# A hybrid decoder layer on one core: side work placed by estimated engine clocks, and gate2 and x1 applied once at the end of the down projection

## The chip, the core and the metric

The kernel runs on one core of one Trainium2 chip. The metric is device time in microseconds (us). Engines are named as in the profile: PE is TensorE, whose weight loads are listed apart as PEld, DVE is VectorE, ACT is ScalarE, POOL is GpSimd, SP is SyncE, which issues most of the DMAs. The kernel before takes 3123.56 us (median of 3 runs, 3122.35 to 3125.27).

## The reference

One inference step of one layer, in float32, for a prompt of 2048 tokens and for 8 sample rows of one token each that share every weight:

```python
h = rmsnorm(x, norm1_g) * (1 + scale1) + shift1          # shift, scale, gate from silu(c) @ w_ada
z = h @ w_in                                             # D = 1024 to 2568 columns
y_a = chunk gating of gelu(z[..., :512]);  y_b = conformer conv of z[..., 512:1024]
y_c = forgetting attention of q, k, v = z[..., 1024:2560], 8 heads of 64
y = concat(rms(y_a), rms(y_b), rms(y_c)) * mix_g
x = x + gate1 * (y @ w_out)
h = rmsnorm(x, norm2_g) * (1 + scale2) + shift2
up = causal depthwise conv3(h @ w_up)                    # 1024 to 2 x 2816
x = x + gate2 * ((silu(up[..., :2816]) * up[..., 2816:]) @ w_down)
return rmsnorm(x, final_g), ...                          # and the new K, V, log-forget and conv rows
```

A sample row attends to 4096 past positions that lie in 32 pages of 128 positions; a page table says where.

## The kernel before

Every large product is made of three float32r matmuls: each operand is split in a high and a low part, and `mm3` (lines 80 to 86) adds high x high, high x low and low x high in PSUM. PSUM is handed out in three tiles `acc` of 128 x 1024 and two tiles `misc` of 128 x 512. The prompt goes in 4 chunks of 512 tokens.

Phase 1 runs, for each chunk, ten groups of columns of `w_in`. Weights come over SP's queue (`raw`), ACT makes the high part `wh`, POOL the low part `wl`. Beside the groups run small tasks, which are Python generators: `norm1` of the next chunk (16 transposes into four `acc` tiles, and for each of eight k a scaling `hmod` and a cast `hh` on ACT and a difference `hl` on DVE), the rest of the adaLN product (`ada_rest`, its weights `wada` issued from ACT's queue), layer norms, gating, row outputs. A task gives up with `yield`, and is taken up again at fixed points: `advance` calls each task once per group, and a number given with `yield` makes it miss so many turns.

Phase 2 is the prompt's attention. In its last quarter `norm_c` normalises the attention's output: squares, four matmuls against ones (128x1), a reciprocal root, four scalings of the identity, one matmul (128x512).

Phase 3 does w_out, norm2, up, down and the final norm, chunk by chunk. A chunk's up projection has 22 tiles of two pieces of weights (48 matmuls each), its down projection has four parts, of 6, 6, 4 and 6 of these tiles. A part is two halves of 512 columns, each with two `acc` tiles. `up` ends a tile with the conv's taps on DVE (four `uy<-ub`, one `uy<-uy`) and the split into `ah` (ACT) and `al` (DVE), which `down` uses as its stationary side. After each half `down` multiplies the sum by gate2 and adds it to `xa`, which holds x1 from the start.

Between them the sample rows' attention goes on. A page step of `logits` (lines 1163 to 1169) takes two pages of K from a ring of four `pg` buffers that SP's queue fills: a product with the query (DVE, `pg<-pg,qb`), a sum by heads (DVE, `red<-pg`), and an addition into the logits `S`. There are 16 steps for each of 8 rows. `values` then takes the maximum, the exponential and the sum (matmuls against `mx`, `dg`, `lsum`) and multiplies 16 x 2 pages of V (tiles `yv` and `pg`) with 32 columns each. How many steps go where is set by numbers: `bg(2)` gives two units of credit, each step costs what its `yield` says, and values of row s-1 and logits of row s take turns.

In a row, L1164 and the like name the line in the listing.

## Time and profile before

| what | value |
|---|---|
| median of 3 runs | 3123.56 us |
| the profiled execution | 3115.85 us, of which 3113.7 us are the span from first to last instruction |
| mean granted PE clock | 0.975 |
| busy share of the span | PE 95%, PEld 69%, DVE 67%, POOL 43%, ACT 39% |
| DMA | 523.90 MB, mean 168 GB/s |

All rows below come from the profiled execution. Busy shares are means over the span: phase 1 ends near 610 us, phase 2 near 1181 us, and the sample rows' page steps stand between 1249 and 2373 us. A wait is idle time of an engine just before an instruction, with what ended it. The granted clock of PE has two levels, 2.4 GHz (1.00) and 1.2 GHz (0.50).

### The profile page before, as it was taken

What the parts mean: (1) busy time and instruction counts of PE and PEld (TensorE: products, weight loads), DVE (VectorE), ACT (ScalarE), POOL (GpSimd) and SP (SyncE); (2) the same over time, 40 slices, a digit from 0 to 9 for tenths busy, and PEclk for the clock granted to TensorE, in tenths of its full rate; (3) what the DMA queues carried; (4) which work ended last, traced back from release to release, by engine and by line L of the source; (5) the groups of instructions that cost most, each with busy time, mean ns of one, the idle gap of its engine ahead of it and who ended that gap; (6) DMA issues with size and microseconds to landing.
All of it is one profiled execution on the core that took longest, in us unless ns stands there. A gap on an engine that the chain in (4) does not pass through costs nothing. (4 is left out here: it accounts for less than half of the span.)

```text
span 3113.7 us, 41614 instructions
## 1 busy us (share of the span) xinstructions
PE 2951.6 (95%) x14352; PEld 2151.2 (69%) x14352; DVE 2087.9 (67%) x2767; ACT 1228.0 (39%) x1717; POOL 1338.4 (43%) x884
## 2 busy tenths in 40 slices
PE   7998989899999989989999999999999999999998
PEld 4776768765555547767776767777767776777775
DVE  4838384858777763986887968785958554645454
ACT  4453535233333343434335433443433433534333
POOL 3544354423333444544444444454444454344443
PEclk9999999999999979999999999999999999999999
DMA  8355756563412327766677787678866627322222
GB/s 260 108 181 171 238 174 205 150 176 80 95 44 63 99 81 281 226 209 200 200 220 236 220 246 212 206 220 284 261 185 191 177 79 235 111 82 82 82 82 78
DMA packets 443589, 523.90 MB, mean 168 GB/s; under 512 B 35111, under 2 KB 281173, under 8 KB 443362
## 3 DMA queue, kind: packets, MB, share of 16 engines
q1 hardware_dynamic: 414418, 478.25, 51.3%
q10 hardware_dynamic: 28672, 41.95, 4.0%
q8 instruction: 113, 1.85, 0.2%
q0 software_dynamic: 288, 1.05, 0.1%
q14 instruction: 98, 0.80, 0.1%
HBM read 453.08 MB, written 68.38 MB: 167 GB/s over the span
## 5 line engine op out<-in xcount | busy, mean ns | idle before, releaser
L1525 POOL TENSOR_TENSOR wl<-raw,wh 128x1024 fp32r<-128x1024 f32 x296 | 769.3, 2609 | 874.9 <-ACT wh L1524 841.9
L84 PE MATMUL acc<-hh,wh 128*128 128x512 f32 x1792 | 721.0, 403 | 3.1 <-ACT hh L451 2.1
L85 PE MATMUL acc<-hl,wh 128*128 128x512 f32 x1792 | 709.4, 396 | 1.8 <-DVE hl L452 1.3
L86 PE MATMUL acc<-hh,wl 128*128 128x512 f32 x1792 | 709.1, 396 | 0.1
L1524 ACT CAST wh<-raw 128x1024 fp32r<-128x1024 f32 x296 | 308.8, 1047 | 552.9 <-PE acc L86 163.7
L1692 DVE SCALAR_TENSOR_TENSOR uy<-ub,fw,uy 128x512 f32<-128x512 f32 x352 | 282.8, 851 | 234.0 <-ACT uy L1689 232.6
L84 PEld LDWEIGHTS acc<-hh,wh 128*128 128x128 f32 x1792 | 338.2, 189 | 127.7 <-issue 22.0
L86 PEld LDWEIGHTS acc<-hh,wl 128*128 128x128 f32 x1792 | 338.4, 189 | 81.5 <-POOL wl L1525 1.0
L85 PEld LDWEIGHTS acc<-hl,wh 128*128 128x128 f32 x1792 | 338.6, 189 | 79.4 <-DVE hl L452 2.1
L496 POOL TENSOR_TENSOR wl<-raw,wh 128x512 fp32r<-128x512 f32 (+1 forms) x160 | 240.1, 1520 | 205.8 <-ACT wh L495 168.7
L84 PE MATMUL acc<-wh,ah 128*128 128x512 f32 x752 | 310.6, 413 | 16.0 <-ACT ah L1698 11.1
L86 PE MATMUL acc<-wh,al 128*128 128x512 f32 x752 | 303.6, 404 | 1.6 <-DVE al L1699 1.6
L85 PE MATMUL acc<-wl,ah 128*128 128x512 f32 x752 | 303.1, 403 | 1.0 <-POOL wl L1525 1.0
L963 POOL TENSOR_TENSOR lsum<-lsum,pt 128x512 f32<-128x512 f32 x96 | 141.0, 1469 | 203.8 <-PE misc L965 102.5
L676 DVE SCALAR_TENSOR_TENSOR cv<-glu,convw,cv 128x512 f32<-128x512 f32 x240 | 226.0, 1004 | 0.0
L1164 DVE TENSOR_TENSOR pg<-pg,qb 128x1024 f32<-128x1024 f32 x128 | 198.4, 1552 | 36.0 <-DMA pg<-in_cache_k 32.7
L995 ACT ACTIVATE pt<-acc 128x1024 f32<-128x1024 f32 (+2 forms) x144 | 126.9, 883 | 240.0 <-PE acc L993 182.5
L84 PEld LDWEIGHTS acc<-wh,ah 128*128 128x128 f32 x752 | 145.7, 194 | 77.1 <-issue 23.9
L84 PE MATMUL acc<-wh,hh 128*128 128x256 f32 (+2 forms) x552 | 163.4, 296 | 9.2 <-DVE nm L871 7.2
L86 PEld LDWEIGHTS acc<-wh,al 128*128 128x128 f32 x752 | 145.3, 193 | 37.9 <-DVE al L1699 3.9
L869 DVE TENSOR_REDUCE nm<-acc 128x1 f32<-128x1024 f32 (+1 forms) x128 | 121.5, 950 | 71.8 <-PE acc L864 71.1
L85 PEld LDWEIGHTS acc<-wl,ah 128*128 128x128 f32 x752 | 145.8, 194 | 32.8 <-POOL wl L1525 1.4
(382 smaller groups left out, 4836.9 us busy)
## 6 DMA issues: line engine op xcount, KB each, us to landing
raw<-in_w_up SPq DMA_DIRECT2D x176, 512.0 KB
pg<-in_cache_k SPq DMA_DIRECT2D x256, 256.0 KB
raw<-in_w_down SPq DMA_DIRECT2D x88, 512.0 KB
yv<-in_cache_v SPq DMA_DIRECT2D x138, 256.0 KB
raw<-in_w_in SPq DMA_DIRECT2D x132, 256.0 KB
pg<-in_cache_v SPq DMA_DIRECT2D x118, 256.0 KB
wada<-in_w_ada ACTq DMA_DIRECT2D x64, 256.0 KB
raw<-in_w_out SPq DMA_DIRECT2D x32, 512.0 KB
```

The source lines that it names most:

```text
L84: nc.tensor.matmul(out, lhsT=lh, rhs=rh, start=start, stop=False)
L85: nc.tensor.matmul(out, lhsT=lh, rhs=rl, start=False, stop=False)
L86: nc.tensor.matmul(out, lhsT=ll, rhs=rh, start=False, stop=stop)
L496: nc.gpsimd.tensor_tensor(out=wl[:, :, 0:n], in0=raw[:, :, 0:n], in1=f(wh[:, :, 0:n]), op=ALU.subtract)
L676: nc.vector.scalar_tensor_tensor(out=y[:, m, :], in0=glu[:, m, j:j + T], scalar=self.convw[:, m, j:j + 1], in1=y[:, m, :], op0=ALU.mult, o ...
L869: nc.vector.tensor_reduce(out=m1, in_=flat[:, 0:full], axis=AX.X, op=ALU.max, negate=True)
L963: e.tensor_tensor(out=lsum[:, i, off:], in0=lsum[:, i, off:], in1=pt[:, i, 0:T - off], op=ALU.add)
L995: nc.scalar.activation(out=pt[:, :, 0:w], in_=ps[:, :, 0:w], func=AF.Exp)
L1164: nc.vector.tensor_tensor(out=t, in0=t, in1=qs[s].unsqueeze(1).broadcast_to([P, 2, 512]), op=ALU.mult)
L1524: nc.scalar.copy(out=wh, in_=raw)
L1525: nc.gpsimd.tensor_tensor(out=wl, in0=raw, in1=f(wh), op=ALU.subtract)
L1692: nc.vector.scalar_tensor_tensor(out=y[:, i, :], in0=ub[:, i, s:s + T], scalar=self.fw[:, s, n:n + 1], in1=y[:, i, :], op0=ALU.mult, op1=A ...
```

## The change

Every engine is wrapped. After each instruction `Estimate.note` adds its estimated cost to a clock of its engine, starting no earlier than the estimated end of what it reads or overwrites; DMAs go to one clock at 280 GB/s. A task now yields a list of what it needs, and is taken up again when the estimate says that this is ready by PE's (or another engine's) clock. Page steps of K run ahead of the values by themselves; they are emitted as long as DVE's clock is less than `lag` behind PE's, 12 us mostly and 3 us in the last two tiles before a down part. `norm1` starts at n == 2 of each chunk as such a task, and what is left of it at the chunk's last group is run off there. The `wada` loads go over SP's queue. V pages use the `yy` ring while it is lent, and `pg` only when no K pages are left. The weights of the next pieces are split before a tile's taps. In the down projection part 0 copies the sum to `xa` (ACT), parts 1 to 3 add to it, and part 3 then multiplies by gate2 and adds x1, which is loaded again as `x1r`. The conformer's layer norm reads a copy in SBUF instead of PSUM.

```diff
+    def cost(self, e, op, outs, ins):
+        n = max(free(x) for x in outs + ins[:1])
+        if e == "tensor":
+            if op == "transpose":
+                return 0.11
+            n = free(ins[1])
+            if "float32r" in str(ins[1].dtype):
+                return max(0.107, 0.0045 + 0.000445 * n)
+            return 4 * max(0.045, 0.00042 * n) * min(1.0, outs[0].shape[0] / 128)
+        if e == "vector":
+            if op == "reciprocal":
+                return 0.1 + 0.0066 * n
+            sb = [x for x in ins if "PSUM" not in str(x.space) and free(x) > 1]
+            return (0.14 + 0.00105 * n) * (1.1 if len(sb) > 1 else 1.0)
+        if e == "scalar":
+            return 0.19 + 0.00083 * n
+        return (1.0 if n < 64 else 0.15) + 0.0023 * n
...
+    def ok(self, need, e="tensor"):
+
+        return not isinstance(need, list) or self.nc.ready(need) <= max(self.nc.t["tensor"], self.nc.t[e]) + 0.1
...
+    def tick(self, n=1):
+
+        for _ in range(n):
+            if self.ok(self.need):
+                self.need = next(self.side, None)
...
-            adas = c in (1, 2) and (c, n) >= (1, 2)
-            if adas:
-                next(ada, None)
+            if (c, n) == (1, 1):
+                self.later(ada)
...
-            if n >= 2:
-                next(nxt, None)
-            if adas:
-                next(ada, None)
+            if n == 2:
+                self.later(nxt)
...
-                self.nc.scalar.dma_start(out=w, in_=self.I["w_ada"][k * P:(k + 1) * P, c0:c0 + 512])
+                self.nc.sync.dma_start(out=w, in_=self.I["w_ada"][k * P:(k + 1) * P, c0:c0 + 512])
...
+    def more(self):
+
+        for _ in range(2):
+            if self.ok(self.wait, "vector"):
+                self.wait = next(self.sample_units, None)
...
             for g in range(NP // 2):
-                t = page()
+                more_k()
+                yield [kt[0], qs[s]]
+                t = kt.pop(0)
...
-            yield 2
+            yield [dg]
...
+        while kn or vs:
+            went = False
+            if vs and self.ok(vn):
+                went = True
+                try:
+                    vn = next(vs)
+                except StopIteration:
+                    vs = None
+            if kn and self.ok(kn, "vector") and (self.force or self.nc.t["vector"] < self.nc.t["tensor"] + self.lag):
+                went = True
+                kn = next(ks, None)
...
-        for _ in range(waits[1]):
-            yield
+        yield [sq, self.acc_free]
...
-                next(self.side, None)
-                if i == 0 and (j != tiles[-1] or len(out) != len(tiles) - 1):
-                    self.bg(2 if c or j > 2 else 0)
+                self.tick()
+                self.lag = 3 if j in tiles[-2:] and tiles[-1] in part else 12
+                if i == 0:
+                    self.more()
...
             for b2 in range(2):
-                t = p3.tile([P, 2, 512], F32, name="t", bufs=2)
-                nc.vector.tensor_tensor(out=t, in0=ps[b2], in1=self.gate[:, 1:2, ns].broadcast_to([P, 2, 512]), op=ALU.mult)
                 xa = self.xa[:, 2 * b2:2 * b2 + 2, ns]
-                nc.vector.tensor_tensor(out=xa, in0=xa, in1=t, op=ALU.add)
+                if n == 0:
+                    nc.scalar.copy(out=xa, in_=ps[b2])
+                else:
+                    nc.vector.tensor_tensor(out=xa, in0=ps[b2], in1=xa, op=ALU.add)
+                if last:
+                    nc.vector.tensor_tensor(out=xa, in0=xa, in1=self.gate[:, 1:2, ns].broadcast_to([P, 2, 512]), op=ALU.mult)
+                    nc.vector.tensor_tensor(out=xa, in0=xa, in1=x1[b2], op=ALU.add)
```

The order of instructions changes on every engine. Every instruction of the kernel after has line L100, that of the wrapper. Three places follow.

The first is ACT's order around norm1 of chunk 1, in phase 1. Before, `hmod` and `hh` of one transposed tile stand among the casts `wh` and outputs of the groups, one tile per group:

```order
L569 COPY sig<-acc 128x1024
L558 ACTIVATE sp_h<-acc 128x1024
L515 COPY zs<-misc 8x256
L561 DMA kh_d<-sp_h 128x2x512
L450 ACTIVATE hmod<-acc,modT,s_226 128x512 x2
L451 CAST hh<-hmod 128x512 x2
L506 COPY part<-misc 128x256
L495 CAST wh<-raw 128x2x256 x4
L558 ACTIVATE sp_h<-acc 128x1024
```

The same in the kernel after, from the output of the chunk's last group (`sp_h`, `qh_d`) on:

```order
L100 ACTIVATE sp_h<-acc 128x1024
L100 ACTIVATE hmod<-acc,modT,s_226 128x512
L100 DMA qh_d<-sp_h 128x2x512
L100 CAST hh<-hmod 128x512
L100 ACTIVATE hmod<-acc,modT,s_226 128x512
L100 CAST wh<-raw 128x2x256
L100 CAST hh<-hmod 128x512
L100 ACTIVATE hmod<-acc,modT,s_226 128x512
L100 COPY part<-misc 128x256
L100 CAST hh<-hmod 128x512
L100 ACTIVATE hmod<-acc,modT,s_226 128x512
L100 COPY zs<-misc 8x256
```

Three of the four tiles' `hmod` and `hh` now stand behind the last group's output, one after the other, where chunk 1's first group needs them.

The second is PE's order where phase 2 ends. Before, the last norm_c stands inside the last attention block, with scores (`acc<-q,k`) between its two steps:

```order
L965 MATMUL misc<-pt,v 64x512 x6
L1487 MATMUL acc<-ones,wk 128x1 x4
L992 MATMUL acc<-q_6414,k_6412 128x512
L993 MATMUL acc<-q_6415,k_6413 128x512
L992 MATMUL acc<-q_6414,k_6412 128x512
L993 MATMUL acc<-q_6415,k_6413 128x512
L1495 MATMUL acc<-wk,ones 128x512
```

After, it stands behind the last block, in front of w_out's first product (`acc<-wh,yy`):

```order
L100 MATMUL misc<-pt,v 64x128 x2
L100 MATMUL acc<-lsum,ones 64x512 x2
L100 MATMUL acc<-ones,wk 128x1 x4
L100 MATMUL acc<-wk,ones 128x512
L100 MATMUL acc<-wh,yy 128x512
L100 MATMUL acc<-wl,yy 128x512
```

Its two steps follow each other directly.

The third is DVE's order in part 2 of chunk 0's down projection, between the second sum of the first half and the first sum of the second. Before, the sums are `t<-acc,gate` and `xa<-xa,t`, and two page steps stand about them:

```order
L1760 TENSOR_TENSOR t<-acc,gate 128x1024
L1168 SCALAR_TENSOR_TENSOR S<-red,S 128x16
L1164 TENSOR_TENSOR pg<-pg,qb 128x1024
L1762 TENSOR_TENSOR xa<-xa,t 128x2x512
L1166 TENSOR_REDUCE red<-pg 128x16
L1168 SCALAR_TENSOR_TENSOR S<-red,S 128x16
L1164 TENSOR_TENSOR pg<-pg,qb 128x1024
L1166 TENSOR_REDUCE red<-pg 128x16
L1760 TENSOR_TENSOR t<-acc,gate 128x1024
```

After, 17 instructions of page steps stand between the two sums `xa<-acc,xa`, the last of them here:

```order
L100 TENSOR_TENSOR pg<-pg,qb 128x1024
L100 TENSOR_REDUCE red<-pg 128x16
L100 SCALAR_TENSOR_TENSOR S<-red,S 128x16
L100 TENSOR_TENSOR pg<-pg,qb 128x1024
L100 TENSOR_REDUCE red<-pg 128x16
L100 SCALAR_TENSOR_TENSOR S<-red,S 128x16
L100 TENSOR_TENSOR xa<-acc,xa 128x2x512
L100 TENSOR_TENSOR pg<-pg,qb 128x1024
L100 TENSOR_REDUCE red<-pg 128x16
L100 TENSOR_TENSOR xa<-acc,xa 128x2x512
```

Counted over DVE's order from the sixth to the 34th `al` (chunk 0's sixth up tile to chunk 1's twelfth), 62 page steps stand there before and 108 after. All 128 stand ahead of the 34th `al` after; before, the last stands behind the 54th.

## Rows read from the trace of the kernel before

**Rows 1.** The page's first part: engine, busy us, share, instructions.
```profile
PE 2951.6 (95%) x14352; PEld 2151.2 (69%) x14352; DVE 2087.9 (67%) x2767; ACT 1228.0 (39%) x1717; POOL 1338.4 (43%) x884
```
**Rows 2.** PE's waits, 60 to 620 us: us in total, times, longest.
```profile
PE misc L255 <- DMA wada<-in_w_ada: 17.2, 5, 7.0
...
PE acc L432 <- ACT vt L590: 5.8, 2, 4.2
PE misc L503 <- ACT part L506: 5.2, 1, 5.2
```
**Rows 3.** Four stretches at the low clock, their sum: length, busy us by engine.
```profile
sum 23.80, PE 14.33 PEld 4.66 DVE 5.19 ACT 20.94 POOL 15.05; mean PE 3.58 PEld 1.17 DVE 1.30 ACT 5.23 POOL 3.76
```
**Rows 4.** ACT's groups, 30 to 620 us: count, busy us, mean ns, idle before.
```profile
L451 ACT CAST hh<-hmod 128x512 fp32r<-128x512 f32 x32 | 19.2, 615 | 1.0 <-DVE hmod L448 0.6
L450 ACT ACTIVATE hmod<-acc,modT,s 128x512 f32<-128x512 f32 x24 | 18.3, 772 | 1.7 <-PE acc L432 1.4 <-ACT zs L515 0.3
```
**Rows 5.** PE's waits over the whole run, norm_c's first step.
```profile
PE acc L1487 <- DVE wk L1481: 7.7, 3, 3.0
```
**Rows 6.** Two stretches at the low clock, 1119.5 to 1140 and 1157 to 1170.7, their sum.
```profile
sum 34.20, PE 29.56 PEld 15.94 DVE 17.36 ACT 9.34 POOL 8.36; mean PE 14.78 PEld 7.97 DVE 8.68 ACT 4.67 POOL 4.18
```
**Rows 7.** PE in order of time, 1157 to 1162 us: start, length, instruction, idle before.
```profile
1157.40 1.84 PE L1487 MATMUL acc<-ones,wk 128*128 128x1 f32 x8 [2.98 <-DVE wk L1481]
...
1161.59 1.19 PE L1495 MATMUL acc<-wk,ones 128*128 128x512 f32 x1 [0.44 <-DVE wk L1491]
```
**Rows 8.** PE's waits, 1181 to 1373 us.
```profile
PE acc L84 <- ACT ah L1698: 7.2, 1, 7.2
```
**Rows 9.** One stretch: busy us (instructions) by engine, granted clock, DMA share, GB/s.
```profile
1365.20:1378.90 13.70, 7.13 (x16) 5.17 (x17) 9.35 (x10) 3.03 (x4) 5.18 (x3) 0.50 1.06 348
```
**Rows 10.** Five stretches between the 6th and the 34th `al`, 1372.9 to 1922.2 us, their sum.
```profile
sum 549.30, PE 532.66 PEld 396.59 DVE 435.83 ACT 220.41 POOL 246.52; mean PE 106.53 PEld 79.32 DVE 87.17 ACT 44.08 POOL 49.30
```
**Rows 11.** DVE's groups, 1372.9 to 1922.2 us.
```profile
L1164 DVE TENSOR_TENSOR pg<-pg,qb 128x1024 f32<-128x1024 f32 x62 | 96.3, 1556 | 27.7 <-DMA pg<-in_cache_k 24.4 <-DMA yv<-in_cache_v 3.3
L1166 DVE TENSOR_REDUCE red<-pg 128x16 f32<-128x1024 f32 x62 | 74.7, 1211 | 0.7
L1168 DVE SCALAR_TENSOR_TENSOR S<-red,S 128x16 f32<-128x16 f32 x61 | 43.6, 719 | 0.7
L1762 DVE TENSOR_TENSOR xa<-xa,t 128x1024 f32<-128x1024 f32 x20 | 32.4, 1619 | 0.2
...
L1760 DVE TENSOR_TENSOR t<-acc,gate 128x1024 f32<-128x1024 f32 x20 | 24.4, 1218 | 16.8 <-PE acc L86 16.8
```
**Rows 12.** A page step's three lines on DVE: ns min/median/max, first and last start.
```profile
L1164 DVE TENSOR_TENSOR pg<-pg,qb x128: 1204/1216/3432, 1249.3 to 2372.9; 128x1024 f32<-128x1024 f32 x128
...
L1166 DVE TENSOR_REDUCE red<-pg x128: 1196/1208/1222, 1258.0 to 2374.2; 128x16 f32<-128x1024 f32 x128
...
L1168 DVE SCALAR_TENSOR_TENSOR S<-red,S x128: 153/168/2416, 1260.3 to 2375.4; 128x16 f32<-128x16 f32 x128
```
**Rows 13.** PE's groups, 1330 to 2540 us: the products with V pages.
```profile
L1205 PE MATMUL misc<-yv,S 128*32 128x512 f32 x276 | 48.1, 598 | 0.1
L1205 PE MATMUL misc<-pg,S 128*32 128x512 f32 x236 | 45.9, 601 | 0.0
```
**Rows 14.** The page's groups: POOL's split of the weights in phase 3.
```profile
L1525 POOL TENSOR_TENSOR wl<-raw,wh 128x1024 fp32r<-128x1024 f32 x296 | 769.3, 2609 | 874.9 <-ACT wh L1524 841.9
```
**Rows 15.** PE's waits, 1922.2 to 3095 us.
```profile
PE misc L1184 <- DVE dg L1181: 7.3, 3, 3.9
...
PE misc L1191 <- DVE lsum L1188: 4.9, 1, 4.9
PE misc L1320 <- DVE ys L1314: 4.2, 1, 4.2
```
**Rows 16.** Four stretches at the low clock between 2273 and 2646 us, their sum.
```profile
sum 20.40, PE 17.11 PEld 14.01 DVE 11.76 ACT 6.75 POOL 10.29; mean PE 4.28 PEld 3.50 DVE 2.94 ACT 1.69 POOL 2.57
```

More of the change, by code (lines that the diff above doesn't have):

```diff
@@ L39, in f, with is_ap, free, __init__ @@
     return ap.bitcast(F32)
+def is_ap(x):
+    return type(x).__name__ == "AP"
+def free(ap):
+    n = 1
+    for _, m in list(ap.ap)[1:]:
+        n *= m
+    return n
+class State:
+    def __init__(self, since):
+        self.since, self.w, self.r, self.last = since, [], [], since
+    def span(self, ap):
+        step = ap.ap[0][0] or 1
+        lo = ap.offset % step if step > 1 else ap.offset
+        return lo, lo + sum((m - 1) * abs(q) for q, m in list(ap.ap)[1:]) + 1
+    @staticmethod
+    def after(items, lo, hi, e="none"):
+        return max((t for a, b, t, by in items if a < hi and lo < b and by != e), default=0.0)
+    def put(self, items, lo, hi, t, e):
+        items[:] = [x for x in items if x[3] != e or not (lo <= x[0] and x[1] <= hi)][-24:] + [(lo, hi, t, e)]
+        self.last = max(self.last, t)
@@ new lines, with __init__, tile, free_at @@
+class Ring:
+    def __init__(self, pool, est, bufs):
+        self.pool, self.est, self.bufs, self.made = pool, est, bufs, {}
+    def tile(self, shape, dtype, **kw):
+        t = self.pool.tile(shape, dtype, **kw)
+        made = self.made.setdefault(kw.get("tag") or kw["name"], [])
+        n = kw.get("bufs") or self.bufs
+        made.append(State(made[-n].last if len(made) >= n else 0.0))
+        self.est.tiles[t.tensor.name] = made[-1]
+        return t
+    def free_at(self, tag, n):
+        made = self.made.get(tag, [])
+        return made[-n].last if len(made) >= n else 0.0
@@ L318, in phase1 @@
                 if c == NCH - 1:
+                    for _ in ada:
+                        pass
+                    self.tasks = [t for t in self.tasks if t[0] is not ada]
                     for name in ("hta", "pa", "px"):
@@ L358, in fill @@
         next(self.filler, None)
+        for t in list(self.tasks):
+            if isinstance(t[1], list) and self.ok(t[1], t[2]):
+                self.step(t)
         if self.taps:
@@ L395, in ada_rest, with square @@
                 ready.append(load(g, k))
-                yield
+                yield list(ready[0])
                 next(gen)
-                yield
-            yield
-            for _ in gen:
-                pass
-            yield
+            yield from gen
+    def square(self, x, out):
+        junk = self.junk.tile([P, D], BF16, name="junk", bufs=1)
+        self.nc.scalar.activation(out=junk, in_=x, func=AF.Square, accum_out=out)
     def norm1(self, c):
@@ L412, in norm1 @@
             nc.sync.dma_start(out=x, in_=I["x_prompt"][t0:t0 + P, :])
-            junk = self.junk.tile([P, D], BF16, name="junk", bufs=1)
-            nc.scalar.activation(out=junk, in_=x, func=AF.Square, accum_out=ssq[:, b:b + 1])
             xs.append(x)
-            if c and b == 1:
-                yield
+            if c and b % 2:
+                yield 1
+            if not c:
+                self.square(x, ssq[:, b:b + 1])
+        if c:
+            for b in range(NB):
+                yield [xs[b]], "scalar"
+                self.square(xs[b], ssq[:, b:b + 1])
         rs = self.small.tile([P, NB], F32, name="rs")
@@ L1415, in phase3 @@
         self.side = self.norm2(0)
-        next(self.side)
+        self.need = next(self.side)
         xa = p3.tile([P, NB, D], F32, name="xa")
@@ L1464, in phase3, with norm_c @@
             self.close(name)
-    def norm_c(self, c, tile, waits=(3, 4, 2, 1)):
+    def norm_c(self, c, tile):
         nc = self.nc
@@ L1473, in norm_c @@
         q, hi = tile(2), tile(3)
-        for _ in range(waits[0]):
-            yield
+        yield ys
         sq = q[:, 0, :]
@@ L1496, in norm_c @@
         nc.scalar.copy(out=sq, in_=ps)
-        for _ in range(waits[3]):
-            yield
+        yield [sq]
         for i in range(2):
@@ L1511, in piece, with ahead @@
     def piece(self):
+        self.ahead(2)
+        self.used += 1
+        return self.split[self.used - 1]
+    def ahead(self, k):
         nc = self.nc
         n = len(self.pieces)
-        while len(self.raws) < min(self.used + 3, n):
+        while len(self.raws) < min(self.used + k + 1, n):
             src = self.pieces[len(self.raws)]
@@ L1547, in y_pair @@
         return [t[:, i, :] for i in range(2)]
-    def page_tile(self, value):
-        for own in (False, True) if value and self.lent else (True,):
-            if self.held[own] < 3:
-                self.held[own] += 1
-                return own, (self.pg if own else self.pw).tile([P, 2, 512], F32, name="pg" if own else "yv", tag="pg" if own else "yy", bufs=4 if own else 3)
     def y_load(self, c, tiles):
@@ L1736, in down @@
             raws = []
+            if last:
+                x1 = [self.pw.tile([P, 2, 512], F32, name="x1r", tag="yy", bufs=3) for _ in range(2)]
+                for b2, x in enumerate(x1):
+                    nc.sync.dma_start(out=x, in_=self.x1_d[c * T + 256 * b2:c * T + 256 * (b2 + 1), ns].rearrange("(b p) d -> p b d", p=P))
             for j in range(0, len(tiles), 2):
-                self.bg(2)
+                self.more()
                 raw, wh, wl = self.piece()
@@ L1744, in down @@
                     if i == 4:
-                        next(self.side, None)
+                        self.tick()
+                        self.more()
                     ah, al = a[j + k]
```

321 lines of the change are left out of this document (198 added, 123 removed).

## The prediction

> **What bounds the kernel now.** I read the page's first part, then PE's waits in three windows, then the stretches at the low clock, then DVE in the stretch where the change puts most of its page steps. The first part says that TensorE is the bound: PE is busy 95% of the span and DVE, the next, 67% [rows 1]. So the change can win only what PE loses now: 162 us of the span (3113.7 - 2951.6), and the stretches in which its clock is granted at 0.50, which is 1.2 GHz, because work there takes twice as long. What the reader is to see in the waits is that they are small and that each has a name: an adaLN weight that comes late, a small result in PSUM that a slow engine has not taken yet, a chain of a sample row's softmax. What the reader is to see in DVE's rows is the other side: its 67% is a mean over stages, and in the densest stretch it is already busy 435.83 of 549.30 us, 79% [rows 10].
>
> The sums are made in the profiled execution (3115.85 us, span 3113.7). The median of the runs is 7.7 us above it; I add the difference that comes out to the median.
>
> **Phase 1: what goes.** PE waits 17.2 us for `wada`, in five waits, because the loads are issued from ACT's queue behind its casts and the products come at a fixed place [rows 2]. With the loads on SP's queue and the task taken up when the estimate has them there, I let three quarters go: -12.9. What they are moved past on SP's queue are `raw` loads of later groups, whose casts wait for PE to free `wh` and `wl`: nothing lost. The wait for `part` (5.2) goes, since its product is now placed after the estimated copy: -5.2. Of the wait for `vt` (5.8), which holds an `acc` tile that norm1 wants, three quarters go: -4.4. Four stretches at the low clock follow these waits; they last 23.80 us and PE is busy 14.33 of it [rows 3], work that takes half of that at 2.4 GHz: -7.2. Together -29.7.
>
> **Phase 1: what comes.** What is left of norm1 at a chunk's last group is run off there. On ACT three of its four tiles' `hmod` and `hh` then stand behind the last output; a tile has two of each, 2 x (0.772 + 0.615) = 2.77 us [rows 4], three tiles 8.3 us. Before, one tile went with each group and the casts of the groups hid it. The cover that is left is PE's last products of the chunk and the groups whose weights are split already. Bounds at each of three boundaries: 0, if PE has so much work queued, and 8.3, if it has none. I take 3, nearer the lower end, since the first tile's half of the contraction lets PE start: +9. Phase 1: -20.7.
>
> **Phase 2.** norm_c's first step waits 7.7 us in three waits [rows 5]; placed by the estimate, half goes: -3.9. The last norm_c loses its cover: the scores that stood between its two steps are gone there, and from the end of the four 128x1 products (1157.40 + 1.84 = 1159.24) to the start of the 128x512 one (1161.59) 2.35 us pass [rows 7], now nearly all idle: +2.4. The low clock around the end of phase 2 lasts 34.20 us with PE busy 29.56 [rows 6]; at 2.4 GHz that is 14.8 less. What PE does before it, waits and small products, is only half removed, so half: -7.4. Phase 2: -8.9.
>
> **Start of phase 3.** PE waits 7.2 us for the first `ah` that a down part needs [rows 8], and the low clock follows (0.50 for 13.70 us, PE busy 7.13 of it, so 3.6 lost) [rows 9]. Now the weights are split ahead of the taps and the lag is cut to 3 us in a part's last tiles, so less stands before `ah`: of 10.8 I take -9.
>
> **The dense stretch, chunk 0's sixth up tile to chunk 1's twelfth.** Here stands the largest term. Its length is 549.30 us, PE is busy 532.66 and DVE 435.83 [rows 10]. The order has 108 page steps there where 62 were. A step costs 1.556 + 1.211 + 0.719 = 3.486 us on DVE in this stretch [rows 11]; 46 more are +160.4. The bare sum gives back: 20 pairs `t<-acc`, `xa<-xa,t` go, 20 x (1.218 + 1.619) = -56.7 [rows 11]. For them come 12 additions from PSUM, each as `t<-acc` (1.218), and in chunk 0's part 3 four products and four sums in SBUF, each as `xa<-xa,t` (1.619): 14.6 + 13.0 = +27.6; the copies of part 0 go to ACT, which is busy 220.41 of 549.30 [rows 10]. So DVE has 435.8 + 160.4 - 56.7 + 27.6 = 567 us of work in a stretch of 549. PE can't pass it: `al`, a product's stationary side, comes from DVE, and behind that stands SP's queue, in which a load of K pages waits until DVE is done with the page buffer and the loads of weights are queued behind it. DVE then sets the end. With no idle time of its own the stretch takes 567 (+18); with all the idle time that its rows show now, 27.7 + 0.7 + 0.7 + 0.2 + 16.8 = 46.1 [rows 11], it takes 613 (+64). I take 574, 7 us of idle time, near the lower end, because a page step that stands ready fills a wait for PE's sums: +25.
>
> The other bound lies below. If a step costs its medians over all 128 (1.216 + 1.208 + 0.168 = 2.592 us) [rows 12], 46 more are 119.2 and DVE has 526 us of work, less than PE's. Then PE decides: its idle time there, 549.30 - 532.66 = 16.6 us, can go, and one sample row's products with V pages, an eighth of 48.1 + 45.9 [rows 13], 11.8 us, move behind the stretch: -28.
>
> Which of the two holds hangs on why mean and median differ. The product `pg<-pg,qb` takes 1216 ns at the median and up to 3432, the small addition `S` 168 and up to 2416, the sum `red` never over 1222 [rows 12]. The excess of 2.2 us is just below one `wl` on POOL, 2609 ns [rows 14]: it is a wait for POOL's split of the weights. The Trainium skill has this rule ("SBUF — State Buffer", section "Who interferes with whom"): a VectorE instruction with two inputs in SBUF shares a port with GpSimd's reads, whoever comes first holds it for its whole instruction and the other blocks, while a reduction never contends; the trace agrees, by the 2.2 us and the reduction that stays at 1222 ns. It speaks against this change, since a placement by fixed prices leaves that out. POOL's work stays, so I take the mean of the stretch.
>
> **Behind it.** The chain waits `dg` 7.3, `lsum` 4.9 and `ys` 4.2 make 16.4 [rows 15]; a task that waits for what it needs should lose three quarters: -12.3. In the low clock there 20.40 us have PE busy 17.11 [rows 16]; 8.6 are lost, half comes back: -4.3. The V products moved out come here: +11.8. Together -4.8. At the end a bank's sum needs one more operation in SBUF after the last product (add, multiply, add, not multiply, add), between 1.2 and 1.6 us, and two banks can't overlap on DVE: +2.5.
>
> **Sum:** -20.7 - 8.9 - 9 + 25 - 4.8 + 2.5 = -15.9, so 3123.6 - 15.9 = 3108 us.
>
> **The rivals.** *DVE never becomes the bound.* For it: steps at the medians, and 12 us of lag let DVE run beside PE. Against it: the mean in just this stretch. The -28 takes the place of the +25: -69, 3055 us. *VectorE becomes the bound, with all its idle time (the other side).* The place is the dense stretch; the price is DVE's 46.1 us of waits for pages and sums that stay, because a page is loaded only when its buffer comes free and the weights' loads stand behind it, so that PE starves and DVE waits for PE in turn. That is +64 in place of +25: +23, 3147 us; with phase 1's bound at 8.3 in place of 3, +39, 3163. It decides as soon as DVE's work with its waits passes 549 + 41, the sum of the gains elsewhere (15.9 + 25). For it: the estimate's own price of a step is 0.14 + 0.00105 n with a tenth on top, 1.34 + 1.215 + 0.17 = 2.73 us by the code, three quarters of a microsecond below the 3.486 that the trace shows, 80 us over 108 steps. Against it: `lag` holds back page steps only on the estimate, yet nearly no step is left after the 34th `al`, so a delay can't grow beyond there. *No gain in phase 1.* Loads of `wada` compete with the `raw` loads on one queue and norm1's remainder costs what the waits cost: phase 1 gives 0 in place of -20.7, and the sum is +4.8, 3128 us.
>
> **How the numbers follow.** A measurement of this kernel can tell 0.2%, 6.2 us, from no change. The forecast has 0.36; its own range is 3094 to 3121 (phase 1's +9 between 0 and 22, the stretch between +18 and +32, rounded), so 0.31 faster and 0.05 same. DVE never the bound: 0.20, all faster. VectorE the bound: 0.32, 0.31 slower and 0.01 same. No gain in phase 1: 0.12, of which 0.01 faster, 0.08 same, 0.03 slower. So faster 0.52, same 0.14, slower 0.34. The range is 3050 to 3165: it reaches to both outer rivals, whose prices rest on the two bounds of one unknown, a page step's cost where it stands dense.
>
> **What would show it.** Right: PE's waits for `wada`, `part` and `vt` all but gone; DVE near 99% busy between the sixth and the 34th `al`, in a stretch of about 575 us, with PE's waits there ended by `al` or by weights; page steps still above 3.2 us; one wait of over 2 us before w_out's first product; waits of PE at the first products of chunks 1 to 3, ended by ACT's `hh` or DVE's `hl`. Wrong: DVE with idle time in the dense stretch and its length near 521 (the first rival), or over 600 with PE waiting for `wl` behind DMA (the second), or `wada` waits as before (the third).

## The result, and the profile after

The kernel after takes 3207.22 us (median of 4 runs, 3197.86 to 3211.47); the kernel before, timed beside it, 3122.95 us (3117.43 to 3125.27, 4 runs). The ratio is 1.0268, with a 95% interval of 1.0241 to 1.0295: slower by 84 us, where 16 us less had been forecast. The profiled execution took 3197.86 us, of which 3196.2 are the span.

The page's first part after, which answers to [rows 1]:

```profile
PE 2986.2 (93%) x14352; PEld 2160.1 (68%) x14352; DVE 2018.6 (63%) x2719; ACT 1242.7 (39%) x1737; POOL 1359.2 (43%) x884
```

By means over the span nothing has become the bound: DVE's share fell from 67% to 63%. The time shows only by stages. The same five stages, cut at the end of the 64th product `acc<-q,k` (the first scores) and of the first, the sixth and the 34th `al`, before and after (columns: stretch, length, busy us of PE, PEld, DVE, ACT and POOL with counts, granted clock, DMA share, GB/s):

```profile
0.00:716.40 716.40, 642.93 (x3791) 505.87 (x3791) 448.03 (x756) 306.13 (x531) 304.00 (x217) 0.97 0.62 185
716.40:1302.70 586.30, 564.98 (x2296) 332.73 (x2296) 426.22 (x685) 205.86 (x266) 234.70 (x191) 0.96 0.40 118
1302.70:1372.90 70.20, 59.43 (x252) 46.40 (x250) 69.33 (x74) 31.68 (x40) 34.97 (x23) 0.95 0.64 211
1372.90:1922.20 549.30, 532.66 (x2341) 396.59 (x2341) 435.83 (x460) 220.41 (x275) 246.52 (x146) 0.98 0.71 215
1922.20:3113.70 1191.50, 1151.62 (x5677) 869.61 (x5676) 708.47 (x797) 463.96 (x606) 518.25 (x310) 0.99 0.52 159
```

```profile
0.00:721.10 721.10, 643.22 (x3791) 508.71 (x3791) 444.22 (x756) 310.25 (x535) 318.08 (x217) 0.96 0.61 183
721.10:1304.20 583.10, 559.17 (x2307) 330.94 (x2307) 427.71 (x679) 207.06 (x269) 236.11 (x193) 0.98 0.39 117
1304.20:1377.50 73.30, 58.19 (x241) 45.31 (x239) 72.33 (x79) 29.18 (x37) 33.65 (x22) 0.93 0.66 205
1377.50:1998.10 620.60, 555.87 (x2270) 403.76 (x2270) 536.16 (x578) 226.78 (x283) 265.37 (x146) 0.94 0.73 218
1998.10:3196.20 1198.10, 1169.80 (x5748) 871.34 (x5747) 538.15 (x631) 469.42 (x615) 505.99 (x309) 0.99 0.48 145
```

The differences are +4.7, -3.2, +3.1, +71.3 and +6.6, together +82.5. Most of it, 71.3, is the dense stretch. PE is idle there 620.6 - 555.9 = 64.7 us, where it was 16.6, and busy 23.2 us longer, though 64 fewer products with V pages stand in it: the granted clock fell from 0.98 to 0.94. DVE is busy 536 us and idle 84. What PE and DVE wait for in that stretch:

```profile
PE acc L100 <- ACT wh L100: 15.5, 4, 7.3
PE acc L100 <- POOL wl L100: 14.3, 11, 2.3
PE misc L100 <- DVE lsum L100: 8.3, 1, 8.3
PE acc L100 <- ACT hh L100: 8.2, 1, 8.2
PE acc L100 <- ACT ah L100: 5.8, 2, 5.0
```

```profile
DVE uy L100 <- ACT uy L100: 31.0, 8, 12.0
DVE pg L100 <- DMA pg<-in_cache_k: 26.0, 11, 5.5
DVE al L100 <- ACT ah L100: 8.4, 12, 0.9
DVE ot L100 <- PE misc L100: 7.1, 1, 7.1
```

PE waits for weights (`wh`, `wl`: 29.8 us), and for results of DVE and ACT. One of the waits in order of time, 1887 to 1908 us: SP's queue (start, length, instructions), then ACT, then PE.

```profile
1887.34 6.63 SPq L100 DMA_DIRECT2D yv<-in_cache_v  x6
1894.81 6.41 SPq L100 DMA_DIRECT2D pg<-in_cache_k  x6
1901.32 2.86 SPq L100 DMA_DIRECT2D raw<-in_w_up  x3
...
1906.36 1.04 ACT L100 CAST wh<-raw 128x1024 fp32r<-128x1024 f32 x1 [12.62 <-DMA raw<-in_w_up]
...
1907.45 0.79 PE L100 MATMUL acc<-hh,wh 128*128 128x512 f32 x1 [7.34 <-ACT wh L100]
```

The load of the weights stands behind twelve page loads. It goes out at 1901, ACT had waited 12.6 us for it, and PE stands still for 7.3.

In phase 1 the waits that the change aims at are mostly gone, and others stand in their place. PE's waits from 60 to 620 us, which answer to [rows 2]:

```profile
PE acc L100 <- POOL vl L100: 13.7, 3, 7.1
PE acc L100 <- ACT ya L100: 12.2, 3, 6.2
...
PE acc L100 <- POOL wl L100: 5.0, 1, 5.0
...
PE misc L100 <- DMA wada<-in_w_ada: 3.5, 1, 3.5
...
PE acc L100 <- ACT vt L100: 0.4, 1, 0.4
```

`wada` fell from 17.2 to 3.5, `vt` from 5.8 to 0.4, and `part` from 5.2 to nothing in this window. `vl` and `ya` are new (25.9 us), and so are `wl`, `carry` (4.9), `lf` (3.3), `sp_l` (2.5) and `cum` (2.3), 18.0 us together. The window doesn't reach the end of phase 1: the last product of its groups ends at 657.7 us before and at 670.8 after, not near 610. `vl` is the gating's layer norm. Before, its products stood two groups behind it; after, they stand where the estimate has it ready, and in chunk 1 that is 7.15 us too early:

```profile
271.99 2.79 POOL L100 TENSOR_TENSOR vl<-vl,bc 128x1024 f32<-128x1024 f32 x1 [4.06 <-DVE vl L100]
...
274.84 2.50 PE L100 MATMUL acc<-vl,wsT 128*128 128x256 f32 x5 [7.15 <-POOL vl L100]
```

The clock falls behind this wait: it is granted at 1.00 from 260.0 to 267.6 us and at 0.57 from 274.8 to 278.2.

### The profile page after: what moved, and what is told of

Read it like the earlier page. It is cut to its first block, busy times and chain, and to the rows that moved or that the text cites. A ratio compares the mean times of both kernels' runs of the same rounds, so it can differ in the third digit from the quotient of the medians.

```text
span 3196.2 us, 41641 instructions
## 1 busy us (share of the span) xinstructions
PE 2986.2 (93%) x14352; PEld 2160.1 (68%) x14352; DVE 2018.6 (63%) x2719; ACT 1242.7 (39%) x1737; POOL 1359.2 (43%) x884
## 5 line engine op out<-in xcount | busy, mean ns | idle before, releaser
L100 POOL TENSOR_TENSOR wl<-raw,wh 128x1024 fp32r<-128x1024 f32 (+2 forms) x456 | 1019.8, 2248 | 1194.0 <-ACT wh L100 1127.4
L100 PE MATMUL acc<-hh,wh 128*128 128x512 f32 x1792 | 729.1, 408 | 28.4 <-ACT hh L100 14.2
L100 PE MATMUL acc<-hh,wl 128*128 128x512 f32 x1792 | 715.4, 400 | 13.0 <-POOL wl L100 13.0
L100 PE MATMUL acc<-hl,wh 128*128 128x512 f32 x1792 | 714.9, 399 | 3.4 <-DVE hl L100 3.4
L100 ACT CAST wh<-raw 128x1024 fp32r<-128x1024 f32 (+2 forms) x456 | 405.3, 896 | 707.9 <-PE acc L100 306.9
L100 DVE SCALAR_TENSOR_TENSOR uy<-ub,fw,uy 128x512 f32<-128x512 f32 x352 | 290.1, 871 | 344.3 <-ACT uy L100 342.6
L100 PEld LDWEIGHTS acc<-hh,wh 128*128 128x128 f32 x1792 | 341.9, 191 | 154.7 <-issue 33.6
L100 PEld LDWEIGHTS acc<-hh,wl 128*128 128x128 f32 x1792 | 341.7, 191 | 101.3 <-POOL wl L100 19.5
L100 PEld LDWEIGHTS acc<-hl,wh 128*128 128x128 f32 x1792 | 342.4, 191 | 82.6 <-DVE hl L100 6.4
L100 PE MATMUL acc<-wh,ah 128*128 128x512 f32 x752 | 307.0, 409 | 22.1 <-ACT ah L100 15.1
L100 PE MATMUL acc<-wh,al 128*128 128x512 f32 x752 | 301.9, 402 | 2.8 <-DVE al L100 2.0
L100 PE MATMUL acc<-wl,ah 128*128 128x512 f32 x752 | 301.5, 401 | 1.3 <-POOL wl L100 1.3
L100 POOL TENSOR_TENSOR lsum<-lsum,pt 128x512 f32<-128x512 f32 x96 | 140.0, 1459 | 200.2 <-ACT pt L100 105.4
L100 DVE SCALAR_TENSOR_TENSOR cv<-glu,convw,cv 128x512 f32<-128x512 f32 x240 | 215.5, 963 | 0.0
L100 ACT ACTIVATE pt<-acc 128x1024 f32<-128x1024 f32 (+2 forms) x144 | 126.6, 882 | 220.8 <-PE acc L100 177.0
L100 PEld LDWEIGHTS acc<-wh,ah 128*128 128x128 f32 x752 | 144.1, 192 | 87.8 <-issue 25.2
L100 DVE TENSOR_TENSOR pg<-pg,qb 128x1024 f32<-128x1024 f32 x128 | 182.8, 1433 | 28.7 <-DMA pg<-in_cache_k 28.7
L100 DVE TENSOR_TENSOR al<-uy,ah 128x512 fp32r<-128x512 f32 x88 | 149.9, 1703 | 51.5 <-ACT ah L100 50.1
L100 PEld LDWEIGHTS acc<-q,k 128*128 128x128 f32 (+1 forms) x640 | 106.3, 190 | 99.1 <-issue 39.3
L100 PE MATMUL acc<-k,q 66*128 66x512 f32 (+7 forms) x640 | 161.6, 373 | 12.3 <-DVE nm L100 11.2
L100 PE MATMUL acc<-q,k 128*128 128x512 f32 (+7 forms) x640 | 171.1, 390 | 1.9 <-DVE nm L100 1.8
L100 PEld LDWEIGHTS acc<-wh,al 128*128 128x128 f32 x752 | 144.0, 191 | 40.1 <-DVE al L100 5.0
```

The source lines that it names most:

```text
L100: res = f(*args, **kw)
```

## The experiments

Three theories. **Theory 1, one queue:** weights stand behind page loads on SP's queue, so PE waits for weights. **Theory 2, DVE's work:** there are too many page steps in front of what PE needs from DVE. **Theory 3, no slack:** a task is placed on PE at the moment when the estimate has its input ready, and the input comes later than that.

In what follows the stretch means that from the 6th to the 34th `al`: 549.3 us before, 620.6 after. Its first part, up to the 28th `al`, holds 48 of the page steps and takes 429.9 us before; after, it holds 85 and takes 484.4. Times stand against the kernel before timed on the same chip, 3120 to 3123 us.

### Weights on ACT's queue

```diff
-            nc.sync.dma_start(out=raw, in_=src)
+            nc.scalar.dma_start(out=raw, in_=src)
```

> The kernel after, with the loads of phase 3's weights (raw) issued from ACT's queue in place of SP's, where page loads wait for DVE. Theory 1 (one queue: weights stand behind page loads on SP's queue): PE's waits for wh and wl in the dense stretch (15.5 + 14.3 us) and the low clock behind them go, 40 to 60 us less, 3150 to 3165 us. Theory 2 (DVE simply has too much work there): taps and ah stay late, 3195 to 3215 us. Theory 3 (tasks are placed on PE with no slack): no change either, 3200 to 3212 us.

Measured: 3220.6 us, ratio 1.0317 (1.0300 to 1.0335), above what any theory expected. The stretch took 603.4 us, 17 less than after, but with 100 page steps in it and not 108. Up to the 28th `al`, with 85 steps as after, it took 485.9 us, no less than after; the gain stands behind that, where 15 steps are left in place of 23 (117.5 us in place of 136.2). PE's waits in the stretch:

```profile
PE acc L100 <- ACT ah L100: 15.8, 2, 11.4
PE acc L100 <- DVE xa L100: 13.6, 2, 7.4
PE acc L100 <- ACT hh L100: 11.2, 1, 11.2
```

The waits for `wh` and `wl` are gone from the stretch, and waits for `ah`, `xa` and `hh` stand in their place. `xa` is DVE's, and `ah` and `hh` are ACT's casts of what DVE makes. ACT itself is held up too, now that it issues the loads: ahead of the longest wait for `ah` it stood 3.31 us for `wl`. So these waits can't be put down to DVE alone by this run. Theory 1 alone falls: PE's waits for weights went and the time didn't. Outside the stretch this edit costs time (the first `al` is 20 us later than after), since ACT's queue waits as well.

### A higher price for DVE

```diff
-            return (0.14 + 0.00105 * n) * (1.1 if len(sb) > 1 else 1.0)
+            return 0.14 + 0.00105 * n + (0.3 if len(sb) > 1 else 0.0)
```

> The kernel after, where the estimate prices a DVE operation with two inputs in SBUF at 0.3 us more in place of a tenth more, about what the trace shows; 105 page steps stand before the 34th al in place of 128. Theory 2: DVE gets what it can do, the dense stretch falls by 40 to 50 us, about 3160 us. Theory 1: fewer page loads in the stretch help half as much, about 3180 us. Theory 3: 3200 us or more.

Measured: 3167.28 us, 1.0134 (1.0114 to 1.0154), 40 us less than after. The stretch took 576.3 us with 85 page steps. Theory 2's number was met in the stretch (44 us less) and nearly met for the whole. Behind the stretch the run lost again: from the 65th to the 67th `al`, around chunk 3's w_out, the loss against before grew from 36 to 51 us.

### Pages loaded but not read

```diff
-                nc.vector.tensor_tensor(out=t, in0=t, in1=q2, op=ALU.mult)
+                nc.vector.real.tensor_tensor(out=ks0, in0=q2, in1=q2, op=ALU.mult)
+                nc.note("vector", "tensor_tensor", (), dict(out=t, in0=t, in1=q2))
...
-                nc.vector.tensor_reduce(out=red, in_=t.rearrange("p a (h d) -> p (a h) d", d=64), axis=AX.X, op=ALU.add)
+                nc.vector.real.tensor_reduce(out=red, in_=ks0.rearrange("p a (h d) -> p (a h) d", d=64), axis=AX.X, op=ALU.add)
```

> The kernel after, where pages of K are loaded as before, but DVE's product reads the query twice and writes a tile of its own, so that no page load waits for DVE and DVE waits for no page (the logits are wrong by that); DVE's work is the same. Theory 1: the dense stretch falls from 620.6 to about 570 us, SP's waits for red (67.8 us) go, 3150 us. Theory 2: DVE's work stays, 3190 us or more.

The tile of its own takes the place of a page buffer: the ring `pg` has three buffers here and not four.

Measured: 3254.45 us in one run, slower still. The stretch took 676.0 us. The steps came in a tighter order (99 of 128 between the 6th and the 28th `al`, 85 after), so the amount of DVE's work in front did not stay as planned, and with a buffer less the run does not part the theories cleanly. Two lines of it are of use. PE's largest waits there are for weights again, and SP's queue now stands in front of page loads that wait for PE (V pages) in place of DVE:

```profile
PE acc L100 <- ACT wh L100: 35.7, 13, 5.2
PE acc L100 <- POOL wl L100: 24.9, 15, 2.6
```

```profile
SPq L100 <- PE misc L100: 82.3, 18, 13.1
SPq L100 <- POOL wl L100: 81.6, 14, 13.6
```

So the weights can be late without DVE's hold on the page buffers.

### Slack for all of PE's tasks

```diff
+        late = -8.0 if e == "tensor" else 0.1
-        return not isinstance(need, list) or self.nc.ready(need) <= max(self.nc.t["tensor"], self.nc.t[e]) + 0.1
+        return not isinstance(need, list) or self.nc.ready(need) <= max(self.nc.t["tensor"], self.nc.t[e]) + late
```

> The kernel after, where a task that PE waits for is taken up only when the estimate has its input ready 8 us before PE's clock. Theory 3: the waits for vl 13.7, ya 12.2, lsum 8.3 and the like and the low clock behind them go, 25 to 40 us less, 3165 to 3180 us, most of it in phase 1; the dense stretch stays within 15 us of 620. Theories 1 and 2: phase 1's share alone is small, 3195 us or more.

Measured: 3320.9 us, 1.0629 (1.0612 to 1.0647): a miss. It began as theory 3 had it: at the end of chunk 1's groups this kernel was 13.2 us ahead of before, where after was 5.4 behind. But at the first scores it was 33.0 us behind before, and at the first `al` 65.2. By the code, tasks that are held back pile up where the program runs off what is left. PE's waits for norm_c's `wk` come to 33.9 us in 5 waits, and from the 65th to the 69th `al`, around chunk 3's w_out, 116 us are lost. The stretch, which was to stay within 15 us of 620, took 582.1 with 101 steps. Slack for every task is no remedy.

### Page steps by a rate

```diff
-            if kn and self.ok(kn, "vector") and (self.force or self.nc.t["vector"] < self.nc.t["tensor"] + self.lag):
+            if kn and self.ok(kn, "vector") and (self.force or len(done) - 1 < 0.12 * (self.nc.t["tensor"] - start)):
...
+                done.append(0)
```

> The kernel after, where page steps of K are held back by a rate, 0.12 a microsecond of PE's estimated clock, and not by DVE's clock: 70 stand between the 6th and the 34th al, against 108 after and 62 before. Theory 2 (too many page steps for DVE): the dense stretch falls from 620.6 to 550 to 565 us, the whole to about 3140 us. Theory 1 (the queue): page loads are spread as well, the same. Theory 3 (no slack): the waits for ah, lsum, hh stay whatever the rate is, 3180 us or more.

Measured: 3216.57 us, 1.0301 (1.0281 to 1.0322). In the stretch theory 2 was right to the number, 560.7 us for 70 steps. The time came back later. From the 66th to the 72nd `al`, around chunk 3's w_out, the run took 238.2 us at a granted clock of 0.92, where the kernel after took 175.9 at 0.99.

The reason, as read from the code, is a line of the change: outside the loan of the `yy` ring, V pages are loaded only `if not kq and not kt`, when no page of K is left. Later steps make later values, and what is left of the sample rows is run off in front of chunk 3. There, 48 products with V pages and two waits of about 10 us (`rows` 10.8, `ys` 9.6) stand on PE. So in this design late page steps have a price of their own. No run changes that line alone.

> The kernel after, with the same hold by a rate, of 0.19 a microsecond: 107 page steps stand between the 6th and the 34th al, one less than after, but evenly by time, whatever DVE's estimated clock says. Theory 2, by the amount: as after, 3195 to 3215 us. If the bursts of the estimate cost the time and not the amount, DVE's 536 us of work fit beside PE's: 3150 us.

The same edit with 0.19 gave 3238.67 us in one run and a stretch of 678.9 us, with 107 steps, one less than after. That is 58 us worse than after, and neither side of the expectation. The steps stand evenly by time, but all 107 stand ahead of the 28th `al`: up to there this run took 552.3 us, with PE's waits for `wh` and `wl` at 35.4 and 35.9 us in the stretch, where after has 85 steps and took 484.4. So it shows again what more steps in front cost, and not what an even order of the same steps would give.

Steps in the stretch and its length: before 62 and 549.3, this hold at 0.12 70 and 560.7, the higher price 85 and 576.3, after 108 and 620.6.

### Cheap steps, and both causes at once

```diff
-                nc.vector.tensor_tensor(out=t, in0=t, in1=qs[s].unsqueeze(1).broadcast_to([P, 2, 512]), op=ALU.mult)
+                t4 = t[:, :, 0:128]
+                nc.vector.real.tensor_tensor(out=t4, in0=t4, in1=qs[s][:, 0:128].unsqueeze(1).broadcast_to([P, 2, 128]), op=ALU.mult)
...
-                nc.vector.tensor_reduce(out=red, in_=t.rearrange("p a (h d) -> p (a h) d", d=64), axis=AX.X, op=ALU.add)
+                nc.vector.real.tensor_reduce(out=red, in_=t4.rearrange("p a (h d) -> p a h d", d=16), axis=AX.X, op=ALU.add)
```

> The kernel after, where a page step's product and sum on DVE run over 128 of 512 columns of a page (the logits are wrong by that), while the estimate still prices the whole; the steps stand at the same places and load the same pages. Theory 2 (DVE's work on the steps in front of what PE needs): the dense stretch falls from 620.6 to 555 to 570 us, the whole to about 3140 us. Theory 1 (transport: page loads, their share of the DMA engines, SP's queue): the stretch stays above 600, 3185 us or more.

Measured: 3153.49 us, 1.0101 (1.0086 to 1.0117), 54 us less than after. The stretch took 593.1 us, between the two expectations, with DVE busy 380 in place of 536, and the same 108 steps. So 27.5 of the 71.3 us that it had grown go with shorter steps. PE's largest waits left:

```profile
PE acc L100 <- ACT wh L100: 15.1, 4, 5.7
PE acc L100 <- POOL wl L100: 8.3, 8, 1.7
```

They are the weights. With this edit and the weights' loads on ACT's queue:

> The kernel after with both edits: a page step's product and sum run over 128 of 512 columns (the logits are wrong by that), and the weights' loads go over ACT's queue. If the stretch is held by two things side by side, DVE's work on the steps and the weights behind page loads on SP's queue, it falls from 593 (cheap steps alone) to 550 to 565 us, the whole to 3115 to 3130 us. If the weights on SP's queue are not the rest, it stays near 593, 3150 us.

Measured: the stretch took 556.6 us, 7.3 more than before, and PE is idle for 556.60 - 535.13 = 21.5 us of it, near the 16.6 of before. But 96 steps stand in it and not 108. The part up to the 28th `al` compares better: after and each edit alone have 85 steps there, both edits 82, and all four have 140 products with V pages. In turn after, the weights on ACT's queue, cheap steps, both:

```profile
1377.50:1861.90 484.40, 433.18 (x1763) 315.84 (x1764) 430.86 (x467) 178.41 (x226) 209.80 (x115) 0.94 0.72 217
```

```profile
1392.20:1878.10 485.90, 428.45 (x1779) 315.72 (x1779) 412.44 (x466) 182.02 (x228) 213.39 (x117) 0.94 0.69 215
```

```profile
1363.70:1828.80 465.10, 429.78 (x1762) 315.79 (x1763) 307.80 (x466) 179.84 (x226) 182.54 (x115) 0.95 0.74 227
```

```profile
1378.00:1812.90 434.90, 414.51 (x1762) 308.34 (x1762) 288.21 (x456) 180.21 (x227) 182.30 (x116) 0.97 0.75 236
```

The other queue alone gives nothing here (+1.5 us), the cheap steps alone give 19.3, and both give 49.5 of the 54.5 us by which this part had grown. PE's waits for `wh` and `wl` in it are 8.2 and 10.5 us after, 13.1 and 6.7 with cheap steps, and none in the two runs with the loads on ACT's queue. That settles this part: two causes side by side, DVE's work on the steps and the weights behind page loads on SP's queue; when one is taken away, the other still comes late. Cheap steps also free the pages earlier: SP's waits for DVE's `red`, `pg` and `S` in the stretch fell from 94.2 to 44.7 us. How much of the 19.3 comes that way stays open.

The whole stayed at 3156.39 us, 1.0121 (1.0101 to 1.0141), so the expectation for the whole was missed: against cheap steps alone, the loads on ACT's queue cost 18.6 us ahead of the first `al` and 18.0 behind the 34th, as much as the stretch gained.

### The other half of the change alone

```diff
+                if n == 0:
+                    nc.scalar.copy(out=xa, in_=ps[b2])
+                else:
+                    nc.vector.tensor_tensor(out=xa, in0=ps[b2], in1=xa, op=ALU.add)
+                if n == 3:
+                    nc.vector.tensor_tensor(out=xa, in0=xa, in1=self.gate[:, 1:2, ns].broadcast_to([P, 2, 512]), op=ALU.mult)
+                    nc.vector.tensor_tensor(out=xa, in0=xa, in1=x1[b2], op=ALU.add)
...
```

Not shown are the loads of `x1r` and the lines that end the loan of the `yy` ring ahead of chunk 0's part 3 and begin it again with chunk 1.

> The kernel before with the bare sum of the down projection alone (part 0 copied by ACT, parts 1 to 3 added, gate2 and x1 in part 3, x1 loaded again into the yy ring). All theories: DVE has about 5 us less work per half chunk outside the path, the tail one operation more: -4 to +3 us, 3119 to 3126 us.

Measured: 3126.2 us, 1.0020 (1.0011 to 1.0029), just above the expected range. The bare sum takes 36 us of work from DVE in the stretch (busy 399.4 of 552.7) and gives nothing: before, PE waited 0.2 us in all for these sums there.

### Phase 1 alone, with and without slack

```diff
+        late = -4.0 if e == "tensor" and self.early else 0.1
...
+            self.early = c < 2
```

> The kernel after, where a task that PE waits for is taken up only when the estimate has its input ready 4 us before PE's clock, in phase 1's chunks 0 and 1 alone. Theory 3: the waits for vl (2.8 and 7.2) and ya (5.2 and 6.2) of these two chunks and the low clock behind them go, phase 1 shorter by 10 to 20 us, 3187 to 3197 us. Theories 1 and 2: nothing changes behind phase 1; if the waits only move to another instruction, 3203 to 3211 us.

Measured: 3190.64 us, 1.0228 (1.0213 to 1.0244), 16.6 us less than after, as theory 3 expected. The first scores came 15.6 us earlier than after. But the waits for `vl` and `ya` in chunks 0 and 1 only fell from 21.4 to 11.5 us, and those in chunks 2 and 3 rose from 4.5 to 13.4; a part of the gain came from other waits (`wl` 5.0, `lf` 3.3 and `cum` 2.3 are gone, `wada` is 0.3).

> Phase 1 as after, phases 2 and 3 as before. If phase 1's own waits (vl, ya) are what the change costs there: +3 to +6 us against before, as the first product of scores stood 4.7 us later in the trace of the kernel after, 3124 to 3128 us. As the prediction had it, -20, 3101 us.

Measured: 3125.31 us, 1.0021 (1.0008 to 1.0034), as expected from phase 1's own waits.

> Phase 1 as after with the 4 us of margin in chunks 0 and 1, phases 2 and 3 as before. Theory 3: phase 1's gain, which stood at 10.8 us at the first scores in the run with the margin, is kept to the end: 3108 to 3113 us, faster than before. If phase 2 or 3 gives it back: 3118 us or more.

Measured: 3115.02 us, 0.9976 (0.9967 to 0.9985): faster than before, but by 5 us in place of 10. In its trace the first scores came 4.9 us ahead of before, so phases 2 and 3 gave nothing back; with the same order of phase 1 the run above had stood 10.9 ahead. The waits for `vl` (11.4) and `ya` (11.8) were still there, 10.2 us of them in chunks 0 and 1 and 13.0 in chunks 2 and 3.

```diff
-        yield [vl, self.acc_free]
+        yield [vl, self.acc_free, lambda: self.nc.ready([vl]) + 6.0]
...
-        yield [y, self.acc_free]
+        yield [y, self.acc_free, lambda: self.nc.ready([y]) + 6.0]
```

> Phase 1 as after, phases 2 and 3 as before, and 6 us of slack in the estimate for two needs alone, vl and ya (yb with it). Theory 3: PE's waits for vl (12.1) and ya (13.5) and the low clock behind them go in all chunks, 20 to 30 us against the run with phase 1 alone (3125), 3095 to 3105 us. If they only move to the next wait: 3115 us or more.

Measured: 3105.3 us, 0.9948 (0.9929 to 0.9968), the fastest of all: 16 us under before and 20 under phase 1 of after alone, by two numbers. PE's waits from 60 to 620 us:

```profile
PE acc L100 <- DVE nm L100: 12.6, 4, 6.5
PE acc L100 <- ACT ya L100: 9.8, 3, 5.0
PE misc L100 <- DMA wada<-in_w_ada: 3.1, 3, 1.6
PE acc L100 <- POOL vl L100: 3.0, 2, 1.8
```

Against phase 1 alone `vl` fell from 12.1 to 3.0 and `ya` only from 13.5 to 9.8; `wl` (4.9) and `carry` (3.3) went with them, and `nm` grew from 7.7 to 12.6. The first scores came at 704.2 us against 720.0 with phase 1 alone and 716.4 before. So theory 3 holds for phase 1: slack on the two needs that come late is enough to turn its loss into a gain, where slack on all was not.

## Why the prediction was wrong

| stage | predicted | measured |
|---|---|---|
| phase 1 | -20.7 | +4.7 |
| phase 2 | -8.9 | -3.2 |
| start of phase 3 | -9 | +3.1 |
| dense stretch | +25 | +71.3 |
| behind it, with the tail | -2.3 | +6.6 |

**The step that failed most** is the idle time in the dense stretch: "I take 574, 7 us of idle time, near the lower end, because a page step that stands ready fills a wait for PE's sums". DVE was idle 620.6 - 536.2 = 84.4 us, more than the upper bound of 46.1. That bound was not all the idle time of before: DVE was busy 435.83 of 549.30 us [rows 10], so it was idle for 113.5, and the five lines of [rows 11] hold 46.1 of that. The other 67.4 were put at nothing without a reason. These two lines hold more than half of it:

```profile
L1692 DVE SCALAR_TENSOR_TENSOR uy<-ub,fw,uy 128x512 f32<-128x512 f32 x112 | 97.8, 930 | 26.9 <-ACT uy L1689 26.8
...
L1699 DVE TENSOR_TENSOR al<-uy,ah 128x512 fp32r<-128x512 f32 x29 | 31.5, 1088 | 9.3 <-ACT ah L1698 9.3
```

The reason that was given isn't borne out. The wait for PE's sums did fall from 16.8 us to 1.2, but with the bare sum alone, at 61 steps in the stretch, it is 0.1, and DVE waits at the taps instead:

```profile
L1698 DVE SCALAR_TENSOR_TENSOR uy<-ub,fw,uy 128x512 f32<-128x512 f32 x112 | 88.6, 849 | 54.6 <-ACT uy L1695 54.6
...
L1772 DVE TENSOR_TENSOR xa<-acc,xa 128x1024 f32<-128x1024 f32 x12 | 14.6, 1214 | 0.1
```

DVE is idle there for 552.7 - 399.4 = 153.3 us. From there to after, whose tasks also stand at other places and which has 47 more steps, its work grows by 137 us; 69 of them went into idle time and 68 into the length of the stretch. A step fills no wait when it waits itself for its page (26.0 us after), or when DVE stands at the taps for ACT's `uy` (31.1).

The mechanism of the loss was written down as the second rival, with PE starving for weights behind page loads, and its sign came: a stretch over 600 us with PE waiting for weights behind DMA. That its 613 us are near the 620.6 measured is luck: it has 31 us too much of DVE's work and 38 too little of its idle time. It had 0.32, the forecast 0.36. What it lacked is the clock: PE's work there took 23.2 us more at a granted 0.94.

**DVE's work** was the smaller error: 567 us predicted, 536 measured. A page step cost 1.445 + 1.213 + 0.430 = 3.09 us, not 3.486 (the sign was to be above 3.2):

```profile
L100 DVE TENSOR_TENSOR pg<-pg,qb 128x1024 f32<-128x1024 f32 x108 | 155.7, 1445 | 26.0 <-DMA pg<-in_cache_k 26.0
L100 DVE TENSOR_REDUCE red<-pg 128x16 f32<-128x1024 f32 x109 | 131.9, 1213 | 1.3
L100 DVE SCALAR_TENSOR_TENSOR uy<-ub,fw,uy 128x512 f32<-128x512 f32 x112 | 112.1, 1054 | 31.1 <-ACT uy L100 31.0
L100 DVE SCALAR_TENSOR_TENSOR S<-red,S 128x16 f32<-128x16 f32 x109 | 46.8, 430 | 1.3
```

The sum over heads stayed at its length and the operations with two inputs in SBUF varied, as the prediction had read it; the taps took 1054 ns in place of 930 in the stretch before. The first rival, DVE never the bound, is out: with cheap steps the stretch is 27.5 us shorter.

**Phase 1: what goes** was right in its parts: 28.2 us of waits became 3.9, where 22.5 were to go. **What comes** was looked for in the wrong place. PE has no wait for `hh` between 60 and 620 us in the profile after, so norm1's remainder at the chunk's end, priced at +9, cost next to nothing there. The new waits came from `vl` and `ya`, 25.9 us, and from five others, 18.0 us, which the prediction put at nothing: it counted which waits a placement by need removes, and not that the same rule takes away two groups of distance (`vl`) or one missed turn (`ya`) where before there was no wait at all. That the run with phase 1 alone gave +4.9 us, and slack on these two alone -20 from there, shows it.

**Phase 2 and the start of phase 3.** The wait between norm_c's last two steps was priced at 2.35 us and measured 6.24; it is nearly all that is left for `wk` (6.4), so the first step's waits, of which half was to go, went whole. The first `ah`, to be early by the split ahead of the taps and the lag of 3 us, came later: 9.3 us of wait in place of 7.2 [rows 8].

```profile
PE acc L100 <- ACT ah L100: 9.3, 1, 9.3
```

```profile
1172.34 2.05 PE L100 MATMUL acc<-wk,ones 128*128 128x512 f32 x2 [6.24 <-DVE wk L100]
1173.40 1.42 PE L100 MATMUL acc<-wh,yy 128*128 128x512 f32 x1
```

**Behind the stretch** the chain waits went nearly as forecast (`ys` 3.3 is left of 16.4), but the V products moved out and PE was busy 18.2 us longer.

**The forecast's own range** doesn't follow from its terms: phase 1's +9 between 0 and 22 and the stretch between +18 and +32 give 3092 to 3128, not 3094 to 3121. The measured time lies beyond both, and beyond the outer bound of 3165.

What stays open: how much of the -3.2 in phase 2 is the later norm_c, and why the weights' loads on ACT's queue cost 18.6 us ahead of the first `al`.

## What to carry to other kernels

A schedule by estimated readiness trades known waits for the estimate's errors: a task placed with no distance pays the error on PE (7.15 us at one `vl`) and again in its clock. Slack on the two needs that came late gained 20 us here, and slack on every need cost 114. Where an engine's idle time before is taken as a bound for a denser schedule, take all of it, and ask of each wait whether the new work can fill it: here 46.1 of 113.5 us were counted. And where one fix brings little, try two at once before the cause is dropped, and compare where the amount of work is the same: up to the 28th `al` the single edits gave nothing and 19 us, and both together 50.

## What was not expected of the hardware

With 108 page steps in the stretch in place of 62, the operations with two inputs in SBUF got shorter at the page steps (`S` 430 ns in place of 719) and longer at the taps (1054 in place of 930), with POOL's `wl` at 2789 ns in place of 2649 in the stretch. The extra time moved between instructions when their order changed; no run here tests what it is made of.
